# Five buffers of weight pairs, deeper rings for v and the gates, and the silu products of q, k, v on VectorE

## The chip, the cores and the metric

The kernel runs on one core of one Trainium2 chip. The metric is device microseconds of one execution. The kernel before takes 1763.55 us, the median of three runs (1762.57 to 1767.99).

## The reference

One layer of a hybrid decoder is computed for a prompt (16 meta tokens and 1024 prompt tokens) and for 8 samples of 8 tokens, with the same weights, all in float32. Cut to what matters here:

```python
p = h @ w_in                                   # 1024 columns in, 3616 out
qkv, _ = causal_conv(qkv_pre, conv_buf, gdn_conv_w)   # depthwise, width 4
qkv = jax.nn.silu(qkv)
q, k, v = split_cols(qkv, ...)                 # 8 heads of 64, q and k are l2-normed
o_a = gdn_chunked(q, k, v, g, beta, S_gdn)     # gated delta rule, chunks of 64, a triangular solve per chunk
o_b = gla_chunked(gq, gk, gv, log_a, S_gla)    # gated linear attention, 4 heads, chunks of 64
o = concat(rms_norm(o_a) * silu(gdn_gate), rms_norm(o_b) * silu(gla_gate))
h = layer_norm(ALPHA * h + o @ w_out)
u = causal_conv(h @ w_up, ...)                 # width 3, 2*2816 columns
h = layer_norm(ALPHA * h + (silu(gate) * value) @ w_down)
```

The states and the last rows of the convolutions are outputs too.

## The kernel before, in words

The activations lie transposed (features on partitions, positions in the free dimension). The 1152 padded positions are cut into three blocks of 384 (48 positions of the first are padding, so its matmuls have 336 columns). The last 64 positions of the third block are the samples.

**A block** (function `block`) computes all of `h @ w_in` for its 384 positions, one projection of 128 columns at a time, and then the two attention groups. The string in `ORDER` writes down the order of its steps: `k` (L1050, eight times: four of k and four of q), `v` (L1053, four times), `q` (q and k of GLA, two each), `V` (all of GLA's v), `d` and `g` (four gates each), `n` (norms and the set-up of the delta rule), `a` and `b` (steps of GLA), `l` (a tile of the first layer norm). Generators interleave the steps by hand, and a scheduler of the framework then orders the instructions of every engine, by the dependences, the buffers that are free and the priorities in `PRIO`. A change of a ring's depth therefore moves instructions of all engines.

**A projection** (`stage`, `project`, `mm3`) splits a weight tile into a high and a low part of the fast float32 format, since one matmul in it isn't exact enough: `hi*hi + hi*lo + lo*hi`, three matmuls for each of eight row tiles, lines L237, L238 and L239. So one projection is 24 matmuls of 128x384. The split is done once, in the first block: a DMA (L224) brings 256 KB into `raw` (three buffers), ScalarE rounds it into `hi` (L208), GpSimd subtracts for `lo` (L209), and the pair, `wp`, half of a projection's weights, is kept in DRAM (a DMA on SP's queue, L228) for the later blocks, which load it (L221). `wp` has `NWP` = 3 buffers. Two of them are one projection.

**q, k and v** (`conv_qkv`): ScalarE copies the projection out of PSUM (L350, L354), VectorE does the convolution in four operations (L377, L379), ScalarE makes the sigmoid in three (L335, L336, L337), and GpSimd multiplies (L381). The three operations of the sigmoid are in `sigmoid`, the product is the last line of `conv_qkv`. The results of k and q lie in `kq` (six buffers of two), those of v in `v` (four buffers, four used by a block), the gates in `sg` (four buffers of two, four used by a block).

**The delta rule's set-up** (`gdn_setup`) is the long serial part of a block: matmuls k k^T and q k^T (L546), masks and decays, then 30 steps on VectorE, two small operations each (L564, L566), that invert 32x32 triangles, transposes (L571, L572), two rounds of 32x32 matmuls (L583, L598), and only then the batches (`gdn_batch`: L630/L631, L643, L662) and the scan over chunks (`gdn_scan`: L699, L710). These matmuls use a quarter or a half of the array (64x64, 128x64). GLA has its own chain of the same kind (L803, L840, L869, L971, L980).

After the three blocks: the output projection (`out_proj`, L1103 to L1119), the second layer norm (`ln1`), and the feed-forward part (`up_conv`, `down`), whose up and down projections use the same three matmuls, with `up` and `dn` as their banks of PSUM.

All DMAs are issued on SP's queue. GpSimd issues none.

## Time and profile before

| | |
|---|---|
| median of three runs | 1763.55 us |
| the profiled execution | 1776.32 us |
| its span, first to last instruction | 1774.1 us |
| TensorE, share of the span with a matmul | 93% |
| VectorE, ScalarE, GpSimd, share of the span busy | 56%, 38%, 39% |
| mean granted clock of TensorE | 0.958 |

The profiled execution is 2.2 us longer than its span, and 12.8 us longer than the median of the runs. A share of busy time is a mean over stages with different limits. The stages are read one by one in the prediction, with a view that cuts the span into windows and gives for each the busy time of each engine, how many instructions ran, the clock that TensorE was granted (1.00 is full speed) and the share of the DMA engines.

### The profile page before, as it was taken

How to read it: one execution, taken by the hardware profiler on the slowest of the kernel's cores; microseconds unless marked ns; L12 is line 12 of the kernel's file. 1: busy time of each engine (PE TensorE's matmuls, PEld its weight loads, DVE VectorE, ACT ScalarE, POOL GpSimd, SP SyncE). 2: the span in 40 equal slices, each digit the busy share in tenths (PEclk: the TensorE clock that was granted, in tenths of full speed). 3: DMA queues.
4: the chain of work that ended last, by engine and by line, in shares of the span. 5: the costliest groups of instructions: out<-in, count | busy, mean ns of one | idle time of the engine just before them, and what ended most of it. 6: DMA issues, size and time to landing. Idle time of an engine off the chain costs nothing.

```text
span 1774.1 us, 30592 instructions
## 1 busy us (share of the span) xinstructions
PE 1658.5 (93%) x11939; PEld 1524.2 (86%) x11939; DVE 986.9 (56%) x2083; ACT 665.6 (38%) x1313; POOL 685.8 (39%) x764
## 2 busy tenths in 40 slices
PE   5787899989899998799998999999999999999997
PEld 4676776879787887689888999999999999999996
DVE  7848854376695877763274464344343434434345
ACT  3444552245632555432144423332332323332332
POOL 4644632143522333552013423433343334333346
PEclk9888897999899998899999999999999999999999
DMA  6778742575774535667681111111111111111112
GB/s 205 235 232 283 248 144 85 172 232 168 216 218 138 154 113 172 227 199 224 203 259 36 49 42 49 43 42 49 40 51 40 52 37 49 42 49 42 43 55 101
DMA packets 190716, 223.53 MB, mean 126 GB/s; under 512 B 23403, under 2 KB 157789, under 8 KB 190573
## 3 DMA queue, kind: packets, MB, share of 16 engines
q1 hardware_dynamic: 190573, 221.59, 40.3%
q8 instruction: 94, 1.54, 0.4%
q14 instruction: 49, 0.40, 0.1%
HBM read 161.84 MB, written 59.70 MB: 125 GB/s over the span
## 4 chain that ended last, share of the span: by engine, by line
PE 75%; DVE 13%; DMA 4%; ACT 3%; POOL 2%; issue 2%; SPq 1%; POOLq 0%; ACTq 0%; DVEq 0%
PE up L237 10%; PE up L239 9%; PE up L238 9%; PE mm L237 5%; PE mm L239 5%; PE dn L239 5%; PE dn L238 5%; PE dn L237 5%; PE mm L238 5%; DVE lw L566 1%; PE gd L662 1%; DVE kq L379 1%; DVE t L564 1%; DVE v L379 1%; PE gd L643 1%
## 5 line engine op out<-in xcount | busy, mean ns | idle before, releaser
L209 POOL TENSOR_TENSOR wp<-wraw,wp 128x512 fp32r<-128x512 f32 x160 | 212.6, 1332 | 362.0 <-ACT wp L208 349.9
L237 PE MATMUL up<-h1hi,wp 128*128 128x352 f32 (+2 forms) x1008 | 332.9, 330 | 0.0
L238 PE MATMUL up<-h1lo,wp 128*128 128x352 f32 (+2 forms) x1008 | 332.1, 330 | 0.0
L239 PE MATMUL up<-h1hi,wp 128*128 128x352 f32 (+2 forms) x1008 | 331.2, 329 | 0.0
L1249 DVE TENSOR_TENSOR acc<-acc,dn 128x364 f32<-128x364 f32 (+1 forms) x216 | 112.4, 531 | 376.1 <-PE dn L239 372.6
L237 PE MATMUL mm<-hhi,wp 128*128 128x384 f32 (+1 forms) x576 | 209.5, 365 | 10.4 <-ACT wp L208 6.3
L239 PE MATMUL mm<-hhi,wp 128*128 128x384 f32 (+1 forms) x576 | 206.0, 358 | 11.4 <-POOL wp L209 11.4
L238 PE MATMUL mm<-hlo,wp 128*128 128x384 f32 (+1 forms) x576 | 203.0, 352 | 0.0
L238 PEld LDWEIGHTS up<-h1lo,wp 128*128 128x128 f32 x1008 | 190.0, 189 | 0.6
L239 PEld LDWEIGHTS up<-h1hi,wp 128*128 128x128 f32 x1008 | 189.9, 188 | 0.1
L237 PEld LDWEIGHTS up<-h1hi,wp 128*128 128x128 f32 x1008 | 189.6, 188 | 0.2
L208 ACT ACTIVATE wp<-wraw 128x512 fp32r<-128x512 f32 x160 | 100.4, 628 | 184.9 <-PE up L239 132.7
L238 PE MATMUL dn<-glo,dwh 128*128 128x364 f32 (+1 forms) x480 | 157.5, 328 | 0.0
L237 PE MATMUL dn<-ghi,dwh 128*128 128x364 f32 (+1 forms) x480 | 155.8, 329 | 0.4 <-ACT dwh L208 0.3
L239 PE MATMUL dn<-ghi,dwl 128*128 128x364 f32 (+1 forms) x480 | 151.2, 328 | 0.1
L237 PEld LDWEIGHTS mm<-hhi,wp 128*128 128x128 f32 x576 | 116.4, 202 | 23.7 <-ACT wp L208 9.2
L239 PEld LDWEIGHTS mm<-hhi,wp 128*128 128x128 f32 x576 | 116.5, 202 | 19.8 <-POOL wp L209 15.1
L238 PEld LDWEIGHTS mm<-hlo,wp 128*128 128x128 f32 x576 | 116.0, 201 | 4.4 <-issue 1.8
L1210 ACT ACTIVATE u<-up 128x352 f32<-128x352 f32 x84 | 38.9, 463 | 199.2 <-PE up L239 199.0
L1222 DVE SCALAR_TENSOR_TENSOR y<-u,fpar,y 128x1104 f32<-128x1104 f32 x44 | 94.5, 2148 | 1.1
L237 PEld LDWEIGHTS dn<-ghi,dwh 128*128 128x128 f32 x480 | 90.1, 188 | 0.9 <-ACT dwh L208 0.5
L238 PEld LDWEIGHTS dn<-glo,dwh 128*128 128x128 f32 x480 | 90.2, 188 | 0.0
(413 smaller groups left out, 3427.4 us busy)
## 6 DMA issues: line engine op xcount, KB each, us to landing
wp<-w SPq DMA_DIRECT2D x144, 512.0 KB
w<-wp SPq DMA_DIRECT2D x72, 512.0 KB
wraw<-in_w_up_dram SPq DMA_DIRECT2D x88, 256.0 KB
wraw<-in_w_in_dram SPq DMA_DIRECT2D x56, 256.0 KB
draw<-in_w_down_dram SPq DMA_DIRECT2D x44, 256.0 KB
hd<-xt SPq DMA_DIRECT2D x9, 512.0 KB
la<-gd SPq DMA_DIRECT2D x24, 192.0 KB
wraw<-in_w_out_dram SPq DMA_DIRECT2D x16, 256.0 KB
```

The lines of the kernel that those rows point to most:

```text
L208: act.activation(out=hi, in_=raw, func=AF.Copy)
L209: pool.tensor_tensor(out=lo, in0=raw, in1=hi.bitcast(F32), op=ALU.subtract)
L237: pe.matmul(ps, lh[0], rh[0], start=first, stop=False)
L238: pe.matmul(ps, lh[0], rh[1], start=False, stop=False)
L239: pe.matmul(ps, lh[1], rh[0], start=False, stop=last)
L379: dve.scalar_tensor_tensor(out=dst, in0=at(i), scalar=tap(i), in1=dst, op0=ALU.mult, op1=ALU.add)
L564: dve.tensor_tensor(out=tv, in0=bc(lw[:, j + 1:32, j:j + 1], 128, n, j), in1=bc(lw[:, j:j + 1, 0:j], 128, n, j), op=ALU.mult)
L566: dve.tensor_tensor(out=lw[:, j + 1:32, 0:j], in0=lw[:, j + 1:32, 0:j], in1=tv, op=ALU.add)
L643: pe.matmul(ps[r, 128 * c:128 * c + 128], xf[r, 6 * p + n0 + c], rbf[r, c], start=True, stop=True)
L1210: act.activation(out=u[:, t0:t0 + n], in_=ps[:, 0:n], func=AF.Copy)
L1222: dve.scalar_tensor_tensor(out=y[:, 0:1104], in0=u[:, 2:1106], scalar=fpar[:, TAPF + 88 + f:TAPF + 89 + f], in1=y[:, 0:1104], op0=ALU.mult ...
L1249: dve.tensor_tensor(out=acc[:, o, c], in0=acc[:, o, c], in1=ps[:, 0:n], op=ALU.add)
```

## The change

Four edits. The scratch that the builder reserves for DMAs whose descriptors an engine writes itself is set to 1 KB. `NWP` goes from 3 to 5 (4 KB more on each partition for each buffer, 8 KB in all), `v` from 4 to 6 buffers (1.5 KB each, 3 KB), `sg` from 4 to 5 (3 KB). The last line of `conv_qkv`, 36 products of 128x384 in the whole kernel, is issued by VectorE and no longer by GpSimd.

```diff
-NLA, NLD, NKQ, NG, NWK, NWP = 6, 1, 6, 6, 2, 3
+NLA, NLD, NKQ, NG, NWK, NWP = 6, 1, 6, 6, 2, 5
...
         e = sigmoid(o)
-        pool.tensor_tensor(out=o, in0=o, in1=e, op=ALU.mult)
+        dve.tensor_tensor(out=o, in0=o, in1=e, op=ALU.mult)
...
     def gates(b, h, c0):
-        g = wk.tile([128, 2, BLK], F32, tag="sg", name="sg", bufs=4)
+        g = wk.tile([128, 2, BLK], F32, tag="sg", name="sg", bufs=5)
...
             elif c == "v":
-                vs.append(t15("v", 4))
+                vs.append(t15("v", 6))
...
-    nc = _bacc.Bacc("TRN2", target_bir_lowering=False, num_devices=1)
+    nc = _bacc.Bacc("TRN2", target_bir_lowering=False, num_devices=1, dynamic_dma_scratch_size=1024)
```

The scheduler answers with another order on every engine. Three places show how.

TensorE, late in the first block's scan of the delta rule: `gd<-la,wkb` is the third matmul of a batch, `gd<-rb,xf` the second, `gdo` the scan, `mm` a projection of the second block. Before, one matmul of a batch and one of a projection take turns:

```order
L237 MATMUL mm_3234<-hhi_3093,wp_3230 128x384
L662 MATMUL gd_2875<-la_1031,wkb_2869 64x128
L238 MATMUL mm_3234<-hlo_3094,wp_3230 128x384
L662 MATMUL gd_2875<-la_1031,wkb_2869 64x128
L239 MATMUL mm_3234<-hhi_3093,wp_3230 128x384
L662 MATMUL gd_2875<-la_1031,wkb_2869 64x128
```

After the change, the same batch (the same `gd_2875`) is in one piece:

```order
L643 MATMUL gd_2852<-rb_2848,xf_1199 64x128 x6
L699 MATMUL gdo_2826<-sv_2638,mq_2639 64x64 x2
L699 MATMUL gdo_2826<-sv_2638,mq_2640 64x64 x2
L662 MATMUL gd_2875<-la_1031,wkb_2869 64x128 x6
L238 MATMUL mm_3324<-wp_3329,hhi_3093 128x512
L239 MATMUL mm_3324<-wp_3329,hlo_3094 128x512
L237 MATMUL mm_3325<-wp_3327,hhi_3093 128x512
```

The batch's six matmuls stood between projection matmuls, and now stand together; the projection beside them is a later one (GLA's v in place of one of GLA's q and k), so the projections are further ahead.

ScalarE, at the first projections of the first block: `wp` are the splits, `u` the copies out of PSUM, `e` the sigmoids. Before, the split of `wp_568` stands behind the copy of `u_500`:

```order
L350 ACTIVATE u_417<-mm_392 128x336
L336 ACTIVATE e_373<-e_373 128x384
L208 ACTIVATE wp_514<-wraw_515 128x512
L337 ACTIVATE e_373<-e_373 128x384
L208 ACTIVATE wp_521<-wraw_522 128x512
L818 ACTIVATE g15_936<-bcm_934 128x384
L821 ACTIVATE gl_939<-bcm_934 128x6
L832 ACTIVATE g15_941<-g15_941 128x384
L350 ACTIVATE u_500<-mm_475 128x336
L208 ACTIVATE wp_568<-wraw_569 128x512
L335 ACTIVATE e_426<-kq_324 128x384
```

After the change, `wp_568` and `wp_575` are split before that copy:

```order
L208 ACTIVATE wp_521<-wraw_522 128x512
L350 ACTIVATE u_417<-mm_392 128x336
L335 ACTIVATE e_373<-kq_324 128x384
L208 ACTIVATE wp_568<-wraw_569 128x512
L336 ACTIVATE e_373<-e_373 128x384
L421 ACTIVATE W_438<-S_435 128x48
L337 ACTIVATE e_373<-e_373 128x384
L422 ACTIVATE W_438<-W_438 128x48
L208 ACTIVATE wp_575<-wraw_576 128x512
L350 ACTIVATE u_500<-mm_475 128x336
L335 ACTIVATE e_426<-kq_324 128x384
```

The splits are two halves, one projection, further ahead of the copies and the sigmoids.

VectorE, in the 30 steps of the second block (`lw`, `t15`), between which the convolutions of the third block's first k and q stand. Before:

```order
L566 TENSOR_TENSOR lw_4327<-lw_4327,t15_4329 128x16x15
L346 COPY u_5844<-hist_181 128x3
L362 COPY u_5783<-ms_5789 128x8x3
L564 TENSOR_TENSOR t15_4329<-lw_4327 128x240
L364 COPY ce_5853<-u_5844 128x3
L377 TENSOR_SCALAR kq_5693<-u_5783,par_161 128x64
```

After:

```order
L566 TENSOR_TENSOR lw_4327<-lw_4327,t15_4329 128x16x15
L377 TENSOR_SCALAR kq_5693<-u_5783,par_161 128x64
L381 TENSOR_TENSOR kq_5693<-kq_5693,e_5749 128x384
L379 SCALAR_TENSOR_TENSOR kq_5814<-u_5844,par_161,kq_5814 128x320
L564 TENSOR_TENSOR t15_4329<-lw_4327 128x240
```

The product L381 stands among the steps of the serial chain, where it stood on GpSimd before.

## The prediction

> **What bounds the kernel now.** The profile's page comes first, for two things. TensorE is the busiest engine, and no DMA goes through GpSimd: there is the queue fed by SP (hardware_dynamic) and those that load instructions.
>
> ```profile
> PE 1658.5 (93%) x11939; PEld 1524.2 (86%) x11939; DVE 986.9 (56%) x2083; ACT 665.6 (38%) x1313; POOL 685.8 (39%) x764
> q1 hardware_dynamic: 190573, 221.59, 40.3%
> q8 instruction: 94, 1.54, 0.4%
> ```
>
> Second, the view by windows, cut at the first matmuls and last scan steps of each block's delta rule. Columns: window and length, busy us of TensorE, weight loads, VectorE, ScalarE and GpSimd (instructions in brackets), granted clock, DMA share, GB/s.
>
> ```profile
> 0.00:42.00 42.00, 21.64 (x104) 16.16 (x105) 30.13 (x90) 15.33 (x31) 18.27 (x33) 1.00 0.64 195
> 42.00:113.00 71.00, 58.91 (x320) 53.01 (x319) 48.30 (x96) 36.95 (x81) 41.32 (x33) 0.86 0.71 233
> 113.00:206.00 93.00, 69.84 (x569) 60.98 (x569) 77.02 (x158) 42.36 (x85) 46.16 (x45) 0.85 0.83 265
> 206.00:351.00 145.00, 144.66 (x1195) 107.91 (x1191) 76.15 (x234) 53.50 (x113) 48.05 (x72) 0.89 0.46 146
> 351.00:444.00 93.00, 86.27 (x574) 79.81 (x575) 61.80 (x162) 44.17 (x93) 37.53 (x42) 0.98 0.64 197
> 444.00:536.00 92.00, 82.52 (x706) 70.79 (x705) 71.11 (x175) 46.99 (x108) 34.91 (x38) 0.94 0.70 208
> 536.00:649.00 113.00, 110.79 (x1092) 91.70 (x1087) 84.68 (x299) 50.63 (x115) 33.69 (x56) 0.98 0.44 135
> 649.00:747.00 98.00, 81.11 (x717) 71.03 (x718) 76.58 (x162) 50.57 (x111) 47.63 (x49) 0.84 0.59 183
> 747.00:867.00 120.00, 119.92 (x1341) 103.92 (x1342) 56.19 (x167) 32.50 (x70) 38.31 (x48) 0.97 0.71 212
> 867.00:966.00 99.00, 85.07 (x564) 80.34 (x561) 55.68 (x115) 36.23 (x71) 22.99 (x26) 0.95 0.55 173
> 966.00:1774.00 808.00, 797.75 (x4799) 788.53 (x4797) 349.24 (x428) 256.33 (x439) 316.95 (x327) 1.00 0.16 49
> ```
>
> The last row is the feed-forward part: 808 us, TensorE full, clock 1.00. The change touches no matmul there and TensorE doesn't wait there, so I put it at zero. Everything happens before 966. Three kinds of stage stand there: set-ups (113 to 206, 444 to 536, 649 to 747), in which VectorE's serial steps set the pace; scans (206 to 351, 536 to 649, 747 to 867), in which TensorE has a matmul in flight all the time; and the way from one to the other.
>
> The scans of the first and second block do the same work, with about as many projection matmuls beside it, but the first takes 145 us and the second 113. Smaller windows show why:
>
> ```profile
> 260.00:277.00 17.00, 17.00 (x93) 10.53 (x92) 12.09 (x34) 7.48 (x15) 3.96 (x3) 0.80 0.29 93
> 277.00:301.00 24.00, 24.00 (x96) 15.26 (x96) 6.77 (x20) 4.72 (x11) 7.15 (x14) 0.51 0.19 60
> 301.00:320.00 19.00, 19.00 (x211) 14.09 (x211) 12.78 (x50) 5.33 (x10) 5.96 (x12) 1.00 0.39 133
> ```
>
> From 277 to 301 us TensorE is "busy" all the time with 96 matmuls, at half clock, and every other engine is nearly idle. TensorE's timeline shows what it does (start, us, line, out<-in):
>
> ```profile
> 272.14 0.34 PE L237 MATMUL mm<-hhi,wp 128*128 128x384 f32 x1
> 272.32 0.34 PE L238 MATMUL mm<-hlo,wp 128*128 128x384 f32 x1
> ...
> 273.47 0.43 PE L662 MATMUL gd<-la,wkb 64*64 64x128 f32 x2
> 273.83 0.45 PE L238 MATMUL mm<-hlo,wp 128*128 128x384 f32 x1
> 274.21 0.43 PE L662 MATMUL gd<-la,wkb 64*64 64x128 f32 x2
> ...
> 282.18 0.69 PE L662 MATMUL gd<-la,wkb 64*64 64x128 f32 x2
> 282.80 0.69 PE L239 MATMUL mm<-hhi,wp 128*128 128x384 f32 x1
> 283.41 0.69 PE L662 MATMUL gd<-la,wkb 64*64 64x128 f32 x2
> ```
>
> Projection matmuls in a row start every 0.18 us (272.14, 272.32). In turns with quarter-array matmuls, one round trip takes 0.74 us (273.47 to 274.21), and 1.23 us at half clock (282.18 to 283.41). Taking turns costs more than the work itself.
>
> **The change, term by term.** "Projection matmuls" are those of L237 to L239; their numbers are counted in the two orders.
>
> *Free edits.* The scratch holds descriptors for DMAs that an engine writes; the page shows none such, so 1 KB costs nothing. The deeper rings of v and gates only remove waits.
>
> *First block, to its scan (42 to 206).* Here the weights are split, and queues in order make them wait. ScalarE's timeline (in brackets the idle time before, and what ended it):
>
> ```profile
> 67.48 0.52 ACT L335 ACTIVATE e<-kq 128x384 f32<-128x384 f32 x1 [3.26 <-DVE kq L379]
> 68.03 0.52 ACT L336 ACTIVATE e<-e 128x384 f32<-128x384 f32 x1
> ...
> 69.22 0.52 ACT L337 ACTIVATE e<-e 128x384 f32<-128x384 f32 x1
> 69.63 1.14 ACT L208 ACTIVATE wp<-wraw 128x512 fp32r<-128x512 f32 x2
> 74.44 0.53 ACT L335 ACTIVATE e<-kq 128x384 f32<-128x384 f32 x1 [3.67 <-DVE kq L379]
> ```
>
> GpSimd's timeline at the same place, and a row of TensorE's waits between 42 and 113 us (us in all, times, longest):
>
> ```profile
> 69.81 1.01 POOL L381 TENSOR_TENSOR kq<-kq,e 128x384 f32<-128x384 f32 x1 [2.84 <-ACT e L337]
> 70.78 3.15 POOL L209 TENSOR_TENSOR wp<-wraw,wp 128x512 fp32r<-128x512 f32 x2
> ...
> PE mm L239 <- POOL wp L209: 7.9, 8, 1.9
> ```
>
> The splits (L208, L209) stand behind a sigmoid and a product that wait for the convolution, and the next projection waits for the splits. With five buffers the splits stand a projection further ahead, and GpSimd's queue has no product between them. TensorE's wait for splits is 7.9 us between 42 and 113 (the last row); I take 5 of it. The raw tiles still have three buffers, which keeps a part. Against it, VectorE has three products and part of a layer norm more between the masks and the end of the 30 steps. What a product costs there comes from L811, the same shape on VectorE:
>
> ```profile
> L381 POOL TENSOR_TENSOR kq<-kq,e x24: 1002/1129/1566, 47.8 to 618.7; 128x384 f32<-128x384 f32 x24
> L811 DVE TENSOR_TENSOR g<-g,g x6: 551/557/558, 44.9 to 649.7; 128x384 f32<-128x384 f32 x6
> L209 POOL TENSOR_TENSOR wp<-wraw,wp x53: 1263/1301/1917, 16.4 to 218.0; 128x512 fp32r<-128x512 f32 x53
> L245 DVE BATCH_NORM_STATS2 st<-xt 128x6 f32<-128x512 f32 x18 | 11.4, 682 | 6.6 <-DMA xt<-in_x_sample_dram 3.7 <-DMA xt<-in_x_prompt_dram 2.1 <-DMA prow<-in_gdn_conv_w_dram 0.7
> L252 DVE TENSOR_SCALAR xt<-xt,mv,rs 128x512 f32<-128x512 f32 x18 | 18.9, 1098 | 2.0 <-POOL rs L250 2.0
> 127.00:197.00 70.00, 50.44 (x299) 45.06 (x299) 63.69 (x130) 32.67 (x68) 34.98 (x29) 0.83 0.86 281
> ```
>
> 0.557 us against 1.129 on GpSimd (medians in ns); 36 of them are 20 us. VectorE is busy 63.7 of 70 us in this stretch, so three products (1.7 us) and, of the layer norm, two each of L245 and L252 (2 x 0.682 + 2 x 1.098 = 3.6 us) add up to 5.3; I take 4. A product also waits for its sigmoid, three operations at a pitch of 0.55 us, some 1.8 us behind its convolution. In the new order all but a few have over 2 us of other work between, so I add nothing for that. Term: -5 + 4 = -1 (from -14, if the splits and the half clock around them go, to +8).
>
> A rule speaks against the move: the Trainium skill, "SBUF — State Buffer", section "Who interferes with whom", says that a VectorE instruction with two SBUF inputs and a GpSimd instruction that reads SBUF share one port pair, and that whoever starts second waits for the whole of the other. By that rule each of 36 products could wait for a split of L209. The rows agree in part: L811 never stretches (551 to 558 ns), while L381 on GpSimd goes from 1002 to 1566.
>
> *First scan (206 to 351).* The orders hold 337 projection matmuls here before and 340 after, but changes between these and quarter- or half-array matmuls fall from 123 to 41. That is 41 round trips less, each 0.74 - 0.18 us for the projection - some 0.13 for the pair alone, so 0.43: 17.6 us at full clock. The half clock costs 24 x 0.49 = 11.8 us and 17 x 0.20 = 3.4. Some of both is the same time, and the chain of batches and scan needs its own. The nearest row is the second block's scan, 113 us with 267 projection matmuls and 31 changes: with 340 it would take 113 + 73 x 0.18 = 126. Term: 126 - 145, and I take -20 (from -8, if only part of the half clock goes, to -30).
>
> The clock has a rule too: the Trainium skill, "TensorE: Matmul & The Clock Gate", section "What's actually happening", gives half clock after an idle window of some 3.4 us. By that rule these 24 us, without any idle, should have run at full clock, no reordering could win the clock back, and the sum would be 15 us less of a gain; the row with 0.51 contradicts it.
>
> *To the second set-up (351 to 444).* Projections done earlier are missing here: 274 in place of 355. At 0.18 us that is 81 x 0.18 = 14.6 us, in a window where TensorE is busy 86 of 93. VectorE, 61.8 of 93, could become late. I take -10 (-17 to 0).
>
> *Second set-up (444 to 536).* Its 30 steps are VectorE's alone:
>
> ```profile
> 484.00:525.00 41.00, 38.37 (x210) 34.03 (x209) 39.17 (x117) 14.47 (x38) 10.45 (x10) 0.99 0.71 218
> ```
>
> VectorE is busy 39.2 of 41 us. The new order puts three products (1.7 us) and ten operations of GLA into it; at L811's 0.56 us these are 5.6. With a stop behind another engine: +8 (from +3, if they fill the 1.8 us and gaps, to +12). GLA's ten are missing later, in a scan where VectorE is busy 85 of 113 us, so nothing comes back.
>
> *The rest.* Second scan: 270 projection matmuls in place of 267, 33 changes in place of 31: 0. Third set-up (649 to 747): 244 in place of 210, 34 x 0.18 = 6 us more, in a window where TensorE stands idle 17 of 98: +3 (0 to +9). Third scan: 240 in place of 279, 7 us less, TensorE in use all the time: -5 (-8 to 0). After it, 350 in place of 369: 3.4 us less, -2 (-5 to +2). GpSimd loses 36 x 1.129 = 41 us; off the path except for the splits counted above.
>
> Sum: -1 - 20 - 10 + 8 + 0 + 3 - 5 - 2 = -27 us. The profiled execution, 1776.32 us, would become 1749.3. It is 12.8 us over the median of the runs; I take the change to be worth the same in both: 1763.55 - 27 = 1736.5 us.
>
> **The rivals.**
>
> *The half clock stays or moves.* Taking turns is not its cause, and the new order has its own thin stretch: the clock is also 0.85, 0.84 and 0.86 in windows without such turns. For it speaks that the clock is the throttle's and not the order's; against it that the only stretch of 24 us at half clock lies exactly where turns are densest. 15 us of the gain are gone: -12, 1751.5 us. This is what the rule of the clock gate, cited above, would make of it. Chance 0.15.
>
> *The chain of the scan hides behind the turns.* The half-array matmuls wait for VectorE's copies anyway, and projections in longer runs (340 in some 20 runs, 17 x 0.18 = 3 us each) hold the next scan step up. Then the first scan gives only -8, the way to the second set-up nothing, the third scan and the end nothing: -1 - 8 + 8 + 3 = +2, 1765.5 us. For it: from 277 to 301 us VectorE, busy 6.8 of 24, waits for TensorE's small matmuls and not the reverse. Against it: the second scan has such runs and takes 113 us. Chance 0.12.
>
> *Slower: VectorE's queue becomes the chain.* Each product waits at VectorE's head for a sigmoid or for a split on GpSimd, and all that is queued behind, the steps L564 and L566 and the copies of the scan, waits too. Price: 36 x 0.557 = 20 us for the products, 12 of the first block behind a split each, 12 x 1.30 = 15.6; less 5 for the splits and 20 for the first scan: +11, 1774.5 us. It decides from where VectorE has less idle time than is added: 2 us in 484 to 525 and 6 in 127 to 197, but 31 in 351 to 444. The port rule of the SBUF page is this mechanism's strongest form. Chance 0.13.
>
> That the change doesn't do what it says is excluded by the orders: the products are on VectorE, and the projections are ahead.
>
> **How the numbers follow.** Forecast -27: chance 0.60, with its own range of 1716 to 1753 (the terms' bounds, +-11, 11, 8, 4, 4, 4 and 3, added as independent, make +-19). With the rivals: 0.15 at 1751.5, 0.12 at 1765.5, 0.13 at 1774.5. The range of 1712 to 1770 leaves out about half of the slower case and a tenth of the forecast's low side. About 0.3%, 5.3 us, is what a measurement of this kernel can tell from no change. Faster by more: 0.60 + 0.15 = 0.75; within: 0.12; slower: 0.13.
>
> **What would show it.** In the profile after: the first scan, from the first L630 to the last L710 of the first block, takes 120 to 132 us in place of 145, without 20 us at half clock in one piece (right) or with them elsewhere (first rival). From the first scan's last L710 to the second block's first L546 it takes some 83 us in place of 93. The second set-up takes some 100. The products on VectorE take 0.55 to 0.6 us; if their mean is near 1, or VectorE idles before L381 for over 5 us in all, the slower case is at work. The feed-forward part stays within 2 us of 808. If the scans are as long as before while the projections are ahead, the chain rival is right.

## The result, and the profile after

| | before | after |
|---|---|---|
| median | 1765.77 us (4 runs, 1762.57 to 1778.86) | 1723.64 us (4 runs, 1721.30 to 1726.12) |
| profiled execution, its span | 1776.32, 1774.1 us | 1721.30, 1719.2 us |
| mean granted clock in it | 0.958 | 0.975 |

The ratio is 0.9736, with a 95% interval of 0.9684 to 0.9787: the change is faster by 42 us. The forecast was 27 us. Between the spans of the profiled executions it is 54.9 us, since the one of before is among the longer runs of its kernel. Over all later runs the kernel before went from 1758.95 us to 1786.69 us, and the granted clock went with it: 0.965 in a run of 1760.45 us, 0.946 in the one of 1786.69 us. Same program, same instructions: what differs is how long TensorE ran at half clock. That turns out to be the thread through this case.

The view by windows of the kernel after, cut at the same first matmuls and last scan steps as before (columns as in the prediction):

```profile
42.00:106.00 64.00, 57.34 (x341) 51.21 (x339) 45.10 (x113) 37.56 (x82) 34.14 (x27) 0.95 0.76 257
106.00:204.00 98.00, 74.02 (x629) 65.53 (x629) 79.28 (x156) 47.40 (x96) 51.35 (x48) 0.90 0.87 278
204.00:327.00 123.00, 118.80 (x1171) 99.07 (x1169) 73.85 (x236) 50.34 (x106) 37.94 (x62) 0.99 0.50 168
327.00:401.00 74.00, 69.97 (x478) 64.35 (x478) 56.60 (x158) 36.08 (x77) 18.07 (x27) 0.98 0.68 206
401.00:491.00 90.00, 86.19 (x750) 75.12 (x749) 72.99 (x193) 50.58 (x115) 27.06 (x35) 0.98 0.69 219
491.00:598.00 107.00, 105.88 (x1080) 89.36 (x1076) 83.91 (x286) 46.42 (x108) 29.46 (x53) 1.00 0.51 152
598.00:704.00 106.00, 89.83 (x768) 79.11 (x766) 84.23 (x186) 54.25 (x121) 48.14 (x49) 0.87 0.62 193
704.00:819.00 115.00, 113.82 (x1321) 97.89 (x1314) 53.33 (x165) 30.46 (x68) 34.76 (x47) 0.97 0.67 203
819.00:911.00 92.00, 82.20 (x547) 77.34 (x547) 55.01 (x114) 36.25 (x69) 24.43 (x24) 0.94 0.52 164
911.00:1719.00 808.00, 798.38 (x4800) 789.16 (x4798) 357.94 (x428) 265.19 (x440) 360.73 (x328) 1.00 0.16 48
```

The last row is the feed-forward part, 808 us again with 4800 matmuls (4799 before). The third row is the first scan: 123 us in place of 145, and its clock is 0.99 in place of 0.89. Smaller windows of the same scan:

```profile
240.00:263.00 23.00, 23.00 (x212) 18.81 (x211) 15.12 (x43) 10.38 (x25) 4.03 (x5) 1.00 0.45 151
263.00:283.00 20.00, 20.00 (x179) 15.77 (x179) 13.11 (x43) 7.68 (x14) 8.06 (x16) 1.00 0.51 177
283.00:303.00 20.00, 20.00 (x230) 17.13 (x225) 13.43 (x51) 5.89 (x11) 4.82 (x11) 1.00 0.53 174
```

There is no stretch like that of before with 96 matmuls in 24 us at a clock of 0.51. TensorE's timeline shows the batch whose new order stands in the section on the change, now in one piece (start, us, line; one matmul of L643 or L662 is two records):

```profile
260.19 0.87 PE L643 MATMUL gd<-rb,xf 64*64 64x128 f32 x12
260.99 0.45 PE L699 MATMUL gdo<-sv,mq 128*64 128x64 f32 x8
261.37 0.87 PE L662 MATMUL gd<-la,wkb 64*64 64x128 f32 x12
262.17 0.51 PE L238 MATMUL mm<-wp,hhi 128*128 128x512 f32 x1
```

Six quarter-array matmuls take 0.87 us. In turns, each of them stood for 0.37 us of TensorE's time, and so did the projection matmul beside it.

The stages, from the first and last matmuls of both traces, in us. The second scan is cut, as in the prediction, at its last step but one (the last comes 4.8 us later before and 4.5 after), and the last stage ends with TensorE's last matmul:

| stage | forecast | before | after | change |
|---|---|---|---|---|
| start to the first batch (L630) | -1 | 206.2 | 203.7 | -2.5 |
| first scan | -20 | 144.8 | 123.3 | -21.5 |
| to the second set-up (L546) | -10 | 93.5 | 74.5 | -19.0 |
| second set-up | +8 | 91.3 | 89.1 | -2.2 |
| second scan | 0 | 113.3 | 107.3 | -6.0 |
| third set-up, and the way to it | +3 | 97.8 | 106.3 | +8.5 |
| third scan | -5 | 120.0 | 115.1 | -4.9 |
| behind it | -2 | 896.9 | 890.2 | -6.7 |
| sum | -27 | | | -54.3 |

### The profile page after: what moved, and what is told of

It is laid out like the page before. It is cut to its first block, busy times and chain, and to the rows that moved or that the text cites. A ratio compares the mean times of both kernels' runs of the same rounds, so it can differ in the third digit from the quotient of the medians.

```text
span 1719.2 us, 30489 instructions
## 1 busy us (share of the span) xinstructions
PE 1617.8 (94%) x11939; PEld 1504.4 (88%) x11939; DVE 990.6 (58%) x2119; ACT 670.6 (39%) x1313; POOL 686.4 (40%) x728
## 4 chain that ended last, share of the span: by engine, by line
PE 71%; DVE 10%; DMA 6%; issue 5%; POOL 3%; ACT 3%; SPq 1%; POOLq 0%; ACTq 0%; DVEq 0%
PE up L237 10%; PE up L238 10%; PE up L239 10%; PE dn L239 5%; PE dn L238 5%; PE dn L237 5%; PE mm L238 4%; PE mm L239 4%; PE mm L237 4%; DMA wraw<-in_w_in_dram 1%; POOL wp L209 1%; DVE kq L379 1%; POOL z L1333 1%; PE gd L662 1%; PE gd L643 1%
## 5 line engine op out<-in xcount | busy, mean ns | idle before, releaser
L209 POOL TENSOR_TENSOR wp<-wraw,wp 128x512 fp32r<-128x512 f32 x160 | 240.3, 1505 | 374.4 <-ACT wp L208 358.4
L237 PE MATMUL up<-h1hi,wp 128*128 128x352 f32 (+2 forms) x1008 | 333.1, 330 | 0.0
L239 PE MATMUL up<-h1hi,wp 128*128 128x352 f32 (+2 forms) x1008 | 331.9, 329 | 0.0
L239 PE MATMUL mm<-hhi,wp 128*128 128x384 f32 (+1 forms) x576 | 199.5, 346 | 14.6 <-POOL wp L209 14.6
L237 PE MATMUL mm<-hhi,wp 128*128 128x384 f32 (+1 forms) x576 | 201.0, 350 | 8.2 <-ACT wp L208 3.8
L238 PE MATMUL mm<-hlo,wp 128*128 128x384 f32 (+1 forms) x576 | 198.0, 344 | 0.0
L239 PEld LDWEIGHTS up<-h1hi,wp 128*128 128x128 f32 x1008 | 190.1, 189 | 0.1
L237 PEld LDWEIGHTS up<-h1hi,wp 128*128 128x128 f32 x1008 | 189.9, 188 | 0.2
L237 PE MATMUL dn<-ghi,dwh 128*128 128x364 f32 (+1 forms) x480 | 154.5, 329 | 0.4 <-ACT dwh L208 0.3
L239 PE MATMUL dn<-ghi,dwl 128*128 128x364 f32 (+1 forms) x480 | 151.1, 328 | 0.1
L239 PEld LDWEIGHTS mm<-hhi,wp 128*128 128x128 f32 x576 | 112.4, 195 | 21.1 <-POOL wp L209 17.7
L237 PEld LDWEIGHTS mm<-hhi,wp 128*128 128x128 f32 x576 | 112.6, 196 | 15.8 <-ACT wp L208 5.9
L209 POOL TENSOR_TENSOR dwl<-draw,dwh 128x512 fp32r<-128x512 f32 x40 | 89.8, 2244 | 60.9 <-ACT dwh L208 60.9
L1222 DVE SCALAR_TENSOR_TENSOR y<-u,fpar,y 128x1104 f32<-128x1104 f32 x44 | 91.3, 2076 | 1.1
L237 PEld LDWEIGHTS dn<-ghi,dwh 128*128 128x128 f32 x480 | 89.8, 188 | 0.9 <-ACT dwh L208 0.5
```

The costliest lines, as they stand in the source:

```text
L209: pool.tensor_tensor(out=lo, in0=raw, in1=hi.bitcast(F32), op=ALU.subtract)
L237: pe.matmul(ps, lh[0], rh[0], start=first, stop=False)
L238: pe.matmul(ps, lh[0], rh[1], start=False, stop=False)
L239: pe.matmul(ps, lh[1], rh[0], start=False, stop=last)
L1222: dve.scalar_tensor_tensor(out=y[:, 0:1104], in0=u[:, 2:1106], scalar=fpar[:, TAPF + 88 + f:TAPF + 89 + f], in1=y[:, 0:1104], op0=ALU.mult ...
```

## The experiments

The theory: the gain is the order on TensorE that the scheduler answers with, above all that projection matmuls and quarter-array matmuls no longer take turns in the first scan. The rivals: GpSimd set free; the room of the rings; half clock that comes whatever the order. Twelve kernels were run. The diffs of e1, e2, e4 and e12 are against the kernel before, those of e3, e5, e6, e8, e10 and e11 against the changed one unless it says otherwise. "Turns" stands for the changes between projection and half- or quarter-array matmuls in the first scan, counted in the order; half clock is summed from the clock records of the profiled execution, up to TensorE's last matmul.

| kernel | projections, turns | first scan | half clock in it | half clock in all | behind third scan | median |
|---|---|---|---|---|---|---|
| before | 337, 123 | 144.8 | 30.7 | 143 | 896.9 | 1770.54 to 1775.98 |
| after | 340, 41 | 123.3 | 3.4 | 82 | 890.2 | 1723.64 |
| e1 products only | 324, 122 | 135.8 | 13.6 | 150 | 926.8 | 1788.87 |
| e2 pairs only | 339, 68 | 136.6 | 17.0 | 102 | 896.5 | 1744.64 |
| e3 pairs and products | 340, 41 | 126.0 | 6.8 | 85 | 891.5 | 1721.36 |
| e4 before, no turns | 326, 47 | 117.6 | 0 | 109 | 926.8 | 1757.98 |
| e5 after, turns back | 371, 141 | 162.8 | 34.2 | 133 | 893.0 | 1742.89 |
| e6 third block on GpSimd | 340, 41 | 124.8 | 3.4 | 99 | 901.2 | 1734.73 |
| e8 four pairs | 346, 47 | 121.0 | 0 | 82 | 892.1 | 1728.19 |
| e10 priority 0 | 335, 37 | 122.7 | 0 | 109 | 893.5 | 1736.33 |
| e11 six pairs | 332, 51 | 118.8 | 3.4 | 147 | 903.0 | 1756.03 |
| e12 products, no turns | 314, 45 | 113.1 | 0 | 113 | 901.1 | 1753.64 |

(The row of before gives its profile, and its median over the runs beside e1 to e4, e5 to e8, e9 to e11 and e12: 1772.93, 1775.98, 1770.54 and 1771.13 us. The changed kernel was run in one set alone, beside a median of before of 1765.77 us, so a difference of a few us between it and a later kernel tells nothing.)

**e1: the products alone.**

```diff
-        pool.tensor_tensor(out=o, in0=o, in1=e, op=ALU.mult)
+        dve.tensor_tensor(out=o, in0=o, in1=e, op=ALU.mult)
```

> Only the 36 products of L381 go to VectorE; the ring of weight pairs stays at 3, v and the gates at 4. My theory (the order of TensorE makes the gain, above all in the first scan): in this order the first scan still holds 324 projection matmuls and 122 changes between them and half- or quarter-array matmuls, so it stays at 140 to 148 us with a piece of over 15 us at half clock, and the whole is within 10 us of the kernel before (ratio 0.994 to 1.006). Rival 1 (GpSimd set free makes the gain, whatever TensorE's order): at least half of the gain is here, 20 us or more (ratio under 0.989). Rival 2 (the products load VectorE's serial chain): the two set-ups get longer by 5 us and more each, and the whole is 8 us slower or worse.

Measured: 1.0123 of before (1.0052 to 1.0193), 16 us slower. Rival 1 is out: by itself, the move off GpSimd gains nothing. But the theory's "within 10 us" fails as well, and so do its 140 to 148 us for the first scan with over 15 us at half clock: it took 135.8 us with 13.6. The loss is as large as rival 2 has it, but its reason isn't the one: the second set-up takes 92.0 us in place of 91.3 and the third, with the way to it, 93.2 in place of 97.8; only the first set-up grew, by 10 us, 4 of which the start ahead of it gave back. The loss lies behind the third scan, 30 us. There the trace holds 5070 matmuls of L237 to L239 in place of 4941. All 129 more belong to the output projection: before, they stood in the third scan and on the way to it, and here they were left for last. First e1, then before, from the third scan's end to the last output projection:

```profile
850.00:946.00 96.00, 85.35 (x537) 80.69 (x535) 45.89 (x87) 23.75 (x46) 11.59 (x16) 0.95 0.82 264
```

```profile
867.00:934.00 67.00, 60.41 (x416) 57.08 (x413) 40.26 (x81) 23.87 (x46) 11.58 (x15) 0.95 0.78 246
```

121 more matmuls cost 29 us there, 0.24 us each, with the DMAs busy at 0.82. Inside the scans e1 saved less than that: it ended the third scan 17 us ahead of before, and lost 30.

**e2: the ring of weight pairs alone.**

```diff
-NLA, NLD, NKQ, NG, NWK, NWP = 6, 1, 6, 6, 2, 3
+NLA, NLD, NKQ, NG, NWK, NWP = 6, 1, 6, 6, 2, 5
...
-    nc = _bacc.Bacc("TRN2", target_bir_lowering=False, num_devices=1)
+    nc = _bacc.Bacc("TRN2", target_bir_lowering=False, num_devices=1, dynamic_dma_scratch_size=1024)
```

> Only the ring of weight pairs goes from 3 to 5 (with the DMA scratch of 1 KB that makes the room); the products stay on GpSimd. The order holds 339 projection matmuls and 68 changes in the first scan, 27 changes more than with all edits (41). My theory, at 0.43 us a change: the first scan takes 123 + 27 x 0.43 = 135 us (130 to 139), and the whole is 25 to 35 us faster than before. The window before the first scan gains no more than 8 us. Rival 1 (GpSimd set free makes the gain): less than half the gain, under 20 us. Rival 3 (the ring takes waits away everywhere and the order is a by-product): the whole gain of 42 us is here, with the first scan as short as with all edits.

Measured: 0.9849 (0.9794 to 0.9905), 28 us faster, with a first scan of 136.6 us. Both as the theory has them, and rival 3, which wanted all 42 us here, is out. The rest of the gain comes only when the two edits stand together: with the products on VectorE the order has 41 turns, and with the ring alone it has 68.

**e3: ring and products, without the deeper rings of v and the gates.** Against the kernel before, the diff is that of e1 and e2 together.

> All but the deeper rings of v and of the gates: weight pairs 5, scratch 1 KB, products on VectorE. TensorE's order is that of the changed kernel, instruction for instruction. My theory: the same time as the changed kernel within 5 us, that is 38 to 48 us faster than before, stage by stage within 3 us. Rival 4 (the deeper rings of v and the gates take waits away that no order shows): 5 us or more of the gain are missing, in the second or third block's projections.

Measured: 0.9712 (0.9666 to 0.9758), a median of 1721.36 us against 1723.64 for the whole change. All stages agree within 3 us. The rings of v and of the gates do nothing here that these runs could tell.

**e4: before, without the turns.**

```diff
-PRIO = [[0, 0, 200], [0, 0, 0], [1000, 0, 700]]
+PRIO = [[0, 0, 300], [0, 0, 0], [1000, 0, 700]]
```

> The kernel before with one number of PRIO changed, [0, 0, 200] to [0, 0, 300]: three buffers of weight pairs, products on GpSimd. The order on TensorE is the same word for word up to the first batch (L630); in the first scan it has 326 projection matmuls and 47 changes in place of 337 and 123. My theory: taking turns is what costs. The first scan takes 145 - 76 x 0.43 - 11 x 0.18 = 110 us at the least and 126 by the second block's row; I expect 120 to 130, with no piece of over 12 us at half clock between 206 and 335 us; the 22 projection matmuls that are missing by the second block's norms come later (+4 us); the whole is 12 to 25 us faster than before. Rival 5 (half clock is the throttle's and comes whatever the order): the first scan takes 137 us or more, with a piece of 15 us or more at half clock, and the whole is within 8 us of the kernel before.

Measured: 0.9923 (0.9882 to 0.9963), 15 us faster, and the first scan takes 117.6 us, a little under what was expected. The same window that ran at 0.51 before, and the scan as a whole:

```profile
206.00:323.00 117.00, 114.68 (x1152) 93.94 (x1147) 75.81 (x232) 51.02 (x111) 47.66 (x70) 1.00 0.54 174
277.00:301.00 24.00, 24.00 (x269) 19.10 (x270) 18.06 (x70) 5.79 (x13) 7.15 (x14) 1.00 0.39 129
```

269 matmuls in place of 96, at a clock of 1.00, with three buffers and the products on GpSimd. So that stretch goes with the turns, and for this scan rival 5 falls; e9 below has the turns by themselves. The 27 us of the scan and another 20 of later stages don't all stay: behind the third scan stand 5075 projection matmuls, and 30 us are given back, as in e1.

**e5: after, with the turns put back.**

```diff
-PRIO = [[0, 0, 200], [0, 0, 0], [1000, 0, 700]]
+PRIO = [[0, 0, 100], [0, 0, 0], [1000, 0, 700]]
```

> The changed kernel with one number of PRIO changed, [0, 0, 200] to [0, 0, 100], which puts the taking of turns back: the order on TensorE is that of the changed kernel up to the first batch (L630), and then the first scan has 371 projection matmuls and 141 changes in place of 340 and 41. My theory (turns cost time, and bring the half clock): 50 round trips of 0.43 us and 31 x 0.18 us more, 21 + 6 us, of which the chain of the scan hides some; I expect the first scan at 138 to 150 us in place of 123, with 10 us or more at half clock between 204 and 350 us, and the way to the second set-up shorter by about 5 us. The whole 8 to 20 us slower than the changed kernel, still 20 to 40 faster than before. Rival 5 (half clock comes whatever the order, and turns are hidden): 123 + 6 = 129 us for the first scan, no piece of over 7 us at half clock, the whole within 5 us of the changed kernel.

Measured: 0.9833 (0.9769 to 0.9897); by medians 19 us slower than the changed kernel. The first scan took 162.8 us, more than expected; this profile is the longest of its four runs (1756.93 us). Two pieces of its scan:

```profile
228.00:250.00 22.00, 20.72 (x115) 11.26 (x112) 8.50 (x24) 5.71 (x12) 5.27 (x8) 0.69 0.07 21
330.00:346.00 16.00, 16.00 (x77) 12.11 (x78) 4.72 (x17) 1.53 (x3) 0.00 (x0) 0.57 0.14 44
```

The picture of before is back: few matmuls, low clock, every other engine nearly idle.

**e6: the third block's products back on GpSimd.**

```diff
-        dve.tensor_tensor(out=o, in0=o, in1=e, op=ALU.mult)
+        (dve if b < 2 else pool).tensor_tensor(out=o, in0=o, in1=e, op=ALU.mult)
```

> The changed kernel, but the 12 products of the third block (they lie in the second set-up and behind it) stay on GpSimd. TensorE's order is the same up to the first of them, inside the second block's 30 steps. This tests the term of the second set-up, which I priced at +8 and which came out at -2. Step as priced (products lengthen VectorE's serial chain): the second set-up, first L546 to first L630 of the second block, falls by 2 to 5 us from 89, and the whole is 3 to 8 us faster than the changed kernel. Rival 2b (a product on GpSimd makes the VectorE operations with two inputs in SBUF wait for it, which costs as much as the product on VectorE): the second set-up stays within 2 us of 89, the stretch of L379 and L566 grows again, and the whole is the same or up to 10 us slower.

Measured: 0.9771 (0.9717 to 0.9824), 1734.73 us, 11 us slower than after. The second set-up takes 91.2 us, no less than with the products on VectorE (89.1), and its 30 steps 43.6 us in place of 43.3. The fall that the step as priced asks for isn't there. Rival 2b isn't shown either: L379 and L566 together take as long in this stage as after the change. The 11 us do not price the products: the order differs from inside the second set-up on, and the second scan (111.9), the third (124.4) and the stretch behind (901.2) got longer, the third set-up shorter (98.9).

**e7: turns by themselves, two quarter-array matmuls to a turn.** The first part of the kernel's work, where `proj_a(n)` and `proj_b(n)` issue n projection matmuls and `pair_b` two matmuls 64x64 with 128 columns:

```python
    proj_a(120)
    for _ in range(60):
        proj_b(1)
        pair_b()
    proj_a(121)
    for _ in range(10):
        proj_b(6)
        for _ in range(6):
            pair_b()
    ...
```

> A kernel that leaves the whole layer out and writes 64 columns of a scratch tile to each output: TensorE alone, without waits inside a run. In order: 120 projection matmuls (128x384) in a row; 60 turns of one such and one pair of quarter-array matmuls (64x64, 128 columns, as L662); 121 in a row; 10 groups of 6 and then 6 pairs; 122 in a row; 60 turns of one 128x128 and one pair; 123 in a row; a pause of some 15 us; 60 turns; a pause; 124 in a row; a pause; 10 groups; 125 in a row. My theory: a turn takes 0.74 us at full clock and 1.23 at half, a matmul in a row 0.18. Over six traces of this case, in windows of 3.41 us, the next window came at half clock after all windows with under 1500 streamed columns, after a third of those with 2750 to 3250, after none with more. A turn streams 384 + 2 x 128 = 640 columns, 2950 in a window at full clock, 1775 at half. So the 60 turns fall to half clock and stay there, those after the pause never leave it (74 us), the turns with 128 columns are at half clock from the second window on, rows and groups come back to full clock within two windows. Rival 5 (only an idle window brings half clock, as the Trainium skill, TensorE: Matmul & The Clock Gate, section What's actually happening, has it): no run of turns falls to half clock, and the turns after the pause are at 0.74 us after two windows.

Measured, the rows for 60 turns and for 10 groups:

```profile
28.00:71.00 43.00, 43.00 (x295) 22.25 (x291) 0.00 (x0) 0.00 (x0) 0.00 (x0) 1.00 0.00 1
93.00:119.00 26.00, 26.00 (x290) 21.95 (x289) 0.00 (x0) 0.00 (x0) 0.00 (x0) 1.00 0.00 1
```

The price is right: 60 turns in 43.9 us, 0.73 each; in groups the same work takes 26.9 us, 0.45 each. The clock stayed at 1.00, against my theory. But the kernel was not what the scan has: its turns hold two quarter-array matmuls (they run beside each other and cost no more than one), so that a window streams some 4100 columns, not the 2950 that I had worked out. The turns behind the pauses were partly put in rows by the framework and tell nothing.

**e9: the same with one quarter-array matmul to a turn, and fewer columns step by step.**

```diff
-        for r, ri in halves:
-            pe.matmul(gd[ri, 0:128], wkb[r], la[r], start=True, stop=True)
+            pe.matmul(gd[64:128, 0:128], wkb[0:64], la[0:64], start=True, stop=True)
```

> A kernel that leaves the whole layer out and writes 64 columns of a scratch tile to each output. e7's turns held two quarter-array matmuls each, where those of the scan hold one; here a turn is one projection matmul and one quarter-array matmul of 128 columns, as L662. In order: 100 projection matmuls in a row; 60 turns; 60 in a row; 10 groups of 6 and 6; 60 in a row; then 40 turns each with 320, 256, 192 and 128 columns in place of 384, with 60 in a row between; a pause of some 15 us in which nothing can run; 60 turns with 384 columns; 60 in a row; a pause; 10 groups; 60 in a row. Price, from e7: 0.73 us a turn at full clock, a group 6 x 0.17 + 6 x 0.11 and two changes, under 2.4 us in place of 4.4. Clock, my theory (it follows the columns streamed in a window of 3.41 us; half under about 2500 to 3250, in the count of the trace, where a quarter-array matmul of 128 columns counts 256): a turn of 384 counts 640 in 0.73 us, 2990 a window, on the edge; 320 columns 2690; 256 columns 2390 or more; 128 columns less. So the turns of 192 and 128 columns fall to half clock, those of 384 may, and after the pause the 60 turns stay at half clock (1.2 us each). Rival 5 (only an idle window brings half clock): none of the ladder's turns falls, and those after the pause are at full clock after two windows.

Measured: a row of projections, 60 turns, groups, turns with 320 and with 128 columns:

```profile
4.00:23.00 19.00, 18.79 (x97) 18.79 (x98) 1.12 (x1) 0.50 (x3) 0.00 (x0) 1.00 0.00 1
24.00:93.00 69.00, 69.00 (x177) 32.32 (x177) 0.00 (x0) 0.00 (x0) 0.00 (x0) 0.54 0.00 0
106.00:132.00 26.00, 26.00 (x175) 21.95 (x174) 0.00 (x0) 0.00 (x0) 0.00 (x0) 1.00 0.00 1
144.00:186.00 42.00, 42.00 (x116) 20.70 (x115) 0.00 (x0) 0.00 (x0) 0.00 (x0) 0.55 0.00 0
304.00:341.00 37.00, 37.00 (x121) 21.03 (x119) 0.00 (x0) 0.00 (x0) 0.00 (x0) 0.57 0.00 0
```

TensorE's timeline at the place where the clock falls:

```profile
28.29 0.43 PE L83 MATMUL gd<-la,wkb 64*64 64x128 f32 x2
28.65 0.44 PE L82 MATMUL mm<-hhi,wp 128*128 128x384 f32 x1
29.03 0.68 PE L83 MATMUL gd<-la,wkb 64*64 64x128 f32 x2
29.64 0.69 PE L82 MATMUL mm<-hhi,wp 128*128 128x384 f32 x1
30.26 0.69 PE L83 MATMUL gd<-la,wkb 64*64 64x128 f32 x2
```

By these rows TensorE is never idle, waits for nobody, and falls to half clock 5 us into the turns; it stays there to their end, and so does every step of the ladder. A turn goes from 0.72 to 1.23 us (29.64 to 30.87, where the next one starts). The groups, the same matmuls in another order, hold full clock. Taking turns alone brings the half clock, with one small matmul to a turn; with two, in e7, it did not. Rival 5 is refuted by the turns at the start; those behind the pause, which the expectation wanted cold throughout, warmed up for 6.8 us first, since the framework put 22 projections in a row ahead of them, and then fell as well.

**e8, e11: four and six buffers of weight pairs**, products on VectorE.

```diff
-NLA, NLD, NKQ, NG, NWK, NWP = 6, 1, 6, 6, 2, 5
+NLA, NLD, NKQ, NG, NWK, NWP = 6, 1, 6, 6, 2, 4
```

(e11 has 6 in place of the 4. Both have four buffers of v and of the gates.)

> Four buffers of weight pairs in place of five, v and the gates at 4, products on VectorE. The order has 346 projection matmuls and 47 changes in the first scan (340 and 41 with five; 324 and 122 with three). My theory: the first scan takes 123 + 6 x 0.18 + 3 x 0.43 = 126 us (121 to 131), no piece over 10 us at half clock in it, and the whole is 30 to 45 us faster than before, within 12 us of the changed kernel. Rival 6 (five buffers are needed for the splits of the first block, and the depth itself makes the gain): the start up to the first batch (L630) is 5 us longer than with five, and less than half of the gain, under 20 us, is left.

Measured: 0.9746 (0.9681 to 0.9811), 48 us faster than before and 5 slower than after, a little more than the theory's 30 to 45. The first scan takes 121.0 us, as it has it. The start up to the first batch takes 208.5 us in place of 203.7, about as rival 6 has it, but rival 6 left under 20 us of the gain, and nearly all of it is here.

> Six buffers of weight pairs in place of five, v and the gates at 4, products on VectorE. The order has 332 projection matmuls and 51 changes in the first scan (340 and 41 with five), 313 in place of 274 on the way to the second set-up. My theory (depth pays by the order that it gives, and that is as good with four and five): the first scan takes 120 to 127 us, the way to the second set-up 39 x 0.24 = 9 us more, since fewer projections were done before, and later stages as much less; the whole is within 8 us of the changed kernel. Rival 6 (the depth itself pays, by splits and loads further ahead): 5 us or more faster than the changed kernel, with a start up to the first batch that is 3 us or more shorter.

Measured: 0.9917 (0.9881 to 0.9952), 32 us slower than after. The first scan (118.8) and the way to the second set-up (85.9, 11 more) are within 3 us of what was expected; the whole is not, and neither theory nor rival has it. The trace has 65 us more at half clock than after's, in pieces from the start to behind the third scan, at 87.6 (17.1 us), 394.8 (10.2), 603.0 (10.2), 688.3 (20.5) and 927.2 (10.2). That goes with the loss; which of these pieces the sixth buffer causes, no run here tells.

**e10: after with priority 0.**

```diff
-PRIO = [[0, 0, 200], [0, 0, 0], [1000, 0, 700]]
+PRIO = [[0, 0, 0], [0, 0, 0], [1000, 0, 700]]
```

> The changed kernel with PRIO [0, 0, 200] set to [0, 0, 0], a candidate that the theory of the turns points to: the first scan holds 335 projection matmuls and 37 changes in place of 340 and 41, the way to the second set-up 283 in place of 274, the second scan 254 in place of 270 and 30 changes in place of 33. My theory: the first scan takes 121 to 125 us, the way to the second set-up 2 us more, the second scan 3 less, and the whole is within 6 us of the changed kernel on either side. If the order away from the turns matters as much as the turns (rival 7), the whole differs by over 8 us although the changes are the same.

Measured: 0.9816 (0.9747 to 0.9886), 13 us slower than after, as rival 7 has it. That isn't shown, though. The two come from different sets, and the intervals of their ratios to before overlap. And 8 of the 20 us between the two profiled executions stand where TensorE's order is still after's, row for row, since the two part only at the first batch. The first projections, e10 and then after:

```profile
82.00:114.00 32.00, 31.41 (x140) 27.42 (x140) 5.61 (x21) 14.10 (x30) 13.78 (x13) 0.63 0.51 174
```

```profile
82.00:106.00 24.00, 22.80 (x142) 19.70 (x142) 5.35 (x21) 14.12 (x30) 13.90 (x14) 0.93 0.68 235
```

The same 140 matmuls take 32 or 24 us: in e10 TensorE fell to half clock at 83.8 us and stayed there for 23.9. Another 8 us are in the third scan (123.0 in place of 115.1).

**e12: e1 without the turns**, the diff of e1 and that of e4.

> The kernel of e1 (products on VectorE, three buffers of weight pairs) with one number of PRIO changed, [0, 0, 200] to [0, 0, 300]. The order is e1's up to the first batch (L630). Then the first scan has 314 projection matmuls and 45 changes in place of 324 and 122, and the third scan 258 projection matmuls in place of 206, so that some 75 fewer are left for after it, where 130 more cost e1 30 us. My theory (the edits pay by the order that the scheduler answers with, not by the room or by the engine): the first scan takes 116 to 126 us in place of 136, the stretch behind the third scan 905 us or less in place of 927, the third scan some 8 us more, and the whole 1735 to 1760 us, 30 to 50 us faster than e1 and faster than before, without a deeper ring. Rival 6 (the depth of the ring pays by itself): 1765 us or more, no faster than before.

Measured: 0.9898 (0.9864 to 0.9932), 35 us faster than e1 and 17 faster than before, with a first scan of 113.1 us, 3 under the theory's range, and 901.1 us behind the third. In the main it is as the theory has it: with three buffers and the products moved, one number that changes the order turns a loss into a gain. It isn't the changed kernel's time: by the profiles 31 us are missing, though its first scan is 10 us shorter. It is longer by 8 us before the first batch, 13 on the way to the second set-up, 6 in it and 11 behind the third scan. So the turns of the first scan are not the whole of the gain. Of all versions only e3, which has the change's own order, is as fast as the change; e8 comes within 5 us.

## Why the prediction was right, and where its steps were off

The gain lies in the forecast's range, but it isn't the sum that was forecast: 42 us by the medians and 54 by the stages, where the sum has 27. Most of the difference stands in two terms, the way to the second set-up (9 us more gain) and the second set-up (10 us more). The range of the forecast alone, 1716 to 1753, doesn't quite follow from +-19 about 1736.5, which gives 1717.5 to 1755.5; nothing hangs on it.

**The bound and the first scan.** Right, and for its reason. -20 was forecast, -21.5 measured; e4 takes the turns out of before and e5 puts them into after, and both move the scan by more than 25 us. (The prediction's sentence that the first two scans hold about as many projection matmuls doesn't fit its own counts, 337 and 267; its sum takes the difference in.) The price was overdrawn in one of its parts: grouping saves 0.73 - 0.45 = 0.28 us a turn (e7), not the 0.43 that I took, since the small matmuls don't shrink to 0.13 us at once. The other part, the half clock, does more: 27 of its us are gone from the scan, 13.6 us at the rate of half.

**The prediction's first rival, the half clock stays or moves.** In the first scan it is refuted by e4 and e9. Elsewhere it isn't: ahead of the first batch, one and the same order had 24 us at half clock in one piece in e10 and none such after the change. The Trainium skill, "TensorE: Matmul & The Clock Gate", section "What's actually happening", gives half clock after an idle window of some 3.4 us; the window of 3.41 us is what the traces show, but e9 falls to half clock without any idle. What the clock follows, as far as these traces show, is how many columns were streamed in the window. I counted them in the twelve traces of whole kernels, up to 960 us, from the matmul records (a quarter-array matmul of 128 columns counts 256). Of the windows at full clock with under 1250 columns, 87 of 87 were followed by half clock; between 2500 and 3000, 38 of 76; between 3000 and 3500, 21 of 96; above 3500, 2 of 2522. Between 1250 and 3500 the count alone doesn't tell. From half clock the edge lies at about the same count. A turn streams 640: some 2950 in a window at full clock, on the edge, and 1800 at half clock, far below it. So turns can fall in any window, and once fallen they don't get out by themselves. That would explain why the kernel before varies as it does from run to run; it was not tested by itself.

**The way to the second set-up, -10, came out at -19.** The term was mis-sized. I took 0.18 us for each of the 81 projection matmuls that are missing, and then less for fear of VectorE. Over the kernels here the stage goes from 68.2 us with 266 projections (e5) to 92.5 with 365 (e4), 0.245 us each: that they cost more because they bring their loads and copies along is my reading and was not tested. VectorE wasn't late: busy 56.6 of 74 us, before 61.8 of 93. Where the missing ones went is in the traces too: 62 more stand ahead of the first batch, 638 in place of 576, nearly all of them beside VectorE's first 30 steps (629 matmuls in the row from 106 to 204 us, 569 before in the one from 113 to 206), where TensorE was busy for 69.8 of 93 us. The start up to the first batch didn't get longer by it as a whole (203.7 us in place of 206.2), though its part from 106 us on grew by 5 us. So most of this work went into TensorE's idle time there.

**The second set-up, +8, came out at -2: the step that failed.** The 30 steps did get longer as priced. First before, then after, the steps L564 on VectorE with their first and last start:

```profile
L564 DVE TENSOR_TENSOR t<-lw x30: 192/370/1174, 486.2 to 522.6; 128x30 f32<-128x30 f32 x2, 128x58 f32<-128x58 f32 x2, 128x84 f32<-128x84 f32 x2, 128x108 f32<-128x108 f32 x2
```

```profile
L564 DVE TENSOR_TENSOR t<-lw x30: 191/358/1071, 435.9 to 479.1; 128x30 f32<-128x30 f32 x2, 128x58 f32<-128x58 f32 x2, 128x84 f32<-128x84 f32 x2, 128x108 f32<-128x108 f32 x2
```

They last 36.4 us before and 43.2 after, +6.8. But the stage has a part ahead of them that I left out, from the first L546 to the first step: 486.2 - 444.5 = 41.7 us before, 435.9 - 401.4 = 34.5 after. There the masks on VectorE wait for the matmuls L546 behind projections. The waits of VectorE up to the steps, before and after:

```profile
DVE la L549 <- PE gd L546: 7.0, 4, 2.9
```

```profile
DVE la L549 <- PE gd L546: 2.6, 1, 2.6
```

And behind the steps, up to the batch, 2 us went as well. The gain ahead of the steps comes with the ring: e2, without the products, has 33.7 us there, and 37.2 us of steps. What makes the steps longer stays open: they take 41.4 us in e1, with the products and three buffers, but 43.6 in e6, where the products of this stage are back on GpSimd.

**The third set-up, +8.5 in place of +3.** VectorE's and GpSimd's timelines of the kernel after, in the third block's steps:

```profile
663.62 0.40 DVE L564 TENSOR_TENSOR t<-lw 128x228 f32<-128x228 f32 x1
...
665.42 2.01 DVE L566 TENSOR_TENSOR lw<-lw,t 128x228 f32<-128x228 f32 x1
...
667.47 1.36 DVE L564 TENSOR_TENSOR t<-lw 128x234 f32<-128x234 f32 x1
```

```profile
665.28 1.90 POOL L1001 TENSOR_TENSOR s<-s,gls 128x1024 f32<-128x1024 f32 x1 [2.77 <-PE glo L999]
667.14 1.43 POOL L209 TENSOR_TENSOR wp<-wraw,wp 128x512 fp32r<-128x512 f32 x1
```

An operation that takes 0.38 to 0.40 us at this shape when GpSimd is idle takes 2.01 when it starts behind one of GpSimd's, and ends 0.25 us behind that one's end; the next one ends 0.26 us behind the split. The 60 operations take 34.0 us in this block, 26.3 before. The term left this out. It is the rule that the prediction cites from the Trainium skill, "SBUF — State Buffer", section "Who interferes with whom", and the traces agree: in the four traces of before, after, e1 and e2, the steps that start while GpSimd is idle are 9 to 10 ns longer than the shortest of their line and shape on average, those that start while it works 638 to 697 ns.

**The slower case, VectorE's queue.** Refuted as a bound, right as a mechanism. Rows of the products on VectorE after the change:

```profile
L381 DVE TENSOR_TENSOR kq<-kq,e 128x384 f32<-128x384 f32 x24 | 17.1, 713 | 4.2 <-ACT e L337 4.2
L381 DVE TENSOR_TENSOR v<-v,e 128x384 f32<-128x384 f32 x12 | 7.7, 640 | 3.1 <-ACT e L337 3.1
```

0.69 us on average, over the 0.55 to 0.6 of the sign that I had named and well under 1, with 7.3 us of idle time ahead, over the 5. But what VectorE took over it got back elsewhere: the convolutions L379 take 86.5 us in all after the change and 98.4 before (that the products on GpSimd had been in their way fits, but was not tested), and VectorE's total busy time is 990.6 us in place of 986.9, not 20 more.

**The start, the scans and the end.** The first block's term, -1, came out at -2.5: TensorE's wait for the splits between 42 us and the first L546 is 4.6 us in place of 7.9. How much of it is the edit's own stays open, since e10, with the same order up to there, shows 8 us of difference at this place. The third scan's -5 came out at -4.9, which is closer than the stage repeats (e10, with five projection matmuls more there, took 8 us longer), so the match is in part luck. The stretch behind it, forecast at -2, came out at -6.7, and the second scan's 0 at -6; for this last no experiment stands, and kernels with about the same counts there took 105 to 118 us. From the last output projection to TensorE's last matmul it takes 830.3 us before and 830.4 after: nothing changed in the feed-forward part.

**The second rival, the chain hides behind the turns.** Out: the first scan fell by the whole forecast.

## What to carry to other kernels

A change of a ring's depth or of an engine is judged by the order that it gives, stage by stage: count how often large and small matmuls take turns, how many matmuls are put off into a stage where nothing covers them, and only then the engines' busy time. Two edits can lose alone and gain together, so the parts of a change are priced together as well as apart. Where TensorE shows "busy" with a low granted clock and the other engines idle, group the small matmuls, or put more streamed columns into each window.

## What the runs showed of the hardware that I had not expected

- TensorE falls to half clock without a moment of idle time, when it streams too few columns in a window of 3.41 us; in these traces it always fell after windows with under 1250, after about half of those with 2500 to 3000, and after 2 of 2522 with more than 3500. Work that is slow at half clock can hold it there: 60 turns took 69 us in e9, of which full clock would have needed 44.
- A turn with two quarter-array matmuls on different quarters (e7) takes the same 0.73 us as with one (e9), and the 60 turns stay at full clock. The second small matmul kept the clock up and cost no time.
- The same program in the same order took 1760 or 1787 us with the granted clock (0.965 and 0.946); a stage of 24 us took 32 in another program (e10) that has the same order up to there. A single profile of such a kernel misplaces gains by that much: the profiled executions showed 55 us here, the medians 42.
